# Seven-product pairs in all gate and up blocks and in six of 22 inner pairs of the down projection

## The chip, the cores and the metric

The kernel runs on one core of a Trainium2 chip. A core has TensorE (matmuls; PE in the profile), VectorE (DVE), ScalarE (ACT), GpSimd (POOL) and SyncE (SP). Each engine works through its own instructions in the order in which the program issues them, and waits on semaphores for the others. Transfers are issued from SP, ACT and POOL. The metric is the device time of one execution in microseconds; lower is better.

## The reference, cut to what matters

One encoder layer on 256 rows with model width 2048. All arithmetic is in float32. The change touches its last stage, the feed-forward block and the final norm:

```python
D_MODEL = 2048; SEQ = 256; D_FF = 5632
def swiglu(h, w_gate_up, w_down):
    gate, up = jnp.split(h @ w_gate_up, 2, axis=-1)
    return (jax.nn.silu(gate) * up) @ w_down
def reference(...):
    ...                                     # four mixers, w_out, cross attention
    x = x + swiglu(rms_norm(x, norm_g[l, 2]), w_gate_up[l], w_down[l])
    return rms_norm(x, final_norm_g)
```

Gate and up are a 256 x 2048 by 2048 x 11264 product, down a 256 x 5632 by 5632 x 2048 product.

## The kernel before, in words

**Precision.** Every float32 operand is held as a high and a low part, each in a reduced matmul format. A product of a 128-row operand with a 128 x 512 piece of weights is three matmuls: high by high, high by low, low by high (`part`, L448 to L451). The data is the stationary operand, the weights are streamed.

**The weight stream.** All weights lie in one array, cut into slabs of 128 x 2048 in the order of use. `Stream.raw` (L95) loads a slab from SP into one of three `raw` buffers (four during gate and up). `make` and `split` (L114 to L160) turn each slab into two parts of 128 x 1024: ScalarE casts the high part `wh` (L120), VectorE subtracts it from the raw slab and writes the low part `wl` (L121). `wh` and `wl` go into pools: three buffers in `wp`, two more in `wp2` during gate and up. A buffer comes free when TensorE has used its part, so VectorE and ScalarE work a few parts ahead of TensorE. `free` (L107) picks the pool; the 44 slabs of down may use `wp` alone.

**Seven products.** Two inner blocks of 128 by two column groups of 512 by two row halves of 128 make a 2 x 2 by 2 x 2 block product: eight block products, or seven with sums of blocks on both sides and additions afterwards (the scheme of Strassen and Winograd). Such a pair is called a unit; `seven` (L52) says which slabs are units. A unit's slab is split in four parts: the first of 512 columns, the others of 1024, and in between VectorE forms the weights' sums in the raw buffer (L150). `left` (L900) forms the data's sums once, `combine` (L929) adds the seven results up.

**Gate and up.** `gate_up` (L890) goes over 11 blocks j of 512 hidden columns. Each block has 8 inner pairs i of 128-blocks, for gate and up at once. `sevens` (L47) names the pairs that are units: none in block 0, (1, 5) in blocks 1 to 3, (1, 3, 5) in blocks 4 to 10. The results of the plain pairs and part of the units' results are summed in PSUM, in four banks of one of the two pools `gbank` and `bank`, which alternate by block; the other pool's four banks hold the units' four further sums. `finish` (L943) adds them, applies silu, multiplies, turns the 128 x 512 results (`store_turned`, L474) and stores them to `hidden` in DRAM by eight transfers a block from POOL (L481).

**Background work.** `combine`, `finish`, `turn`, `fetch` and others are generators in a list (`Background`). After each product the planner polls them; a step is issued only when its due time has come and VectorE owes less than 0.9 us by the planner's count. At fixed points a generator is drained, that is run to its end on the spot. So these steps' places in the engines' queues follow from how busy VectorE is by that count; a layer below may issue an instruction earlier where its inputs are ready.

**Fetch and turn.** `fetch` (L874) loads tiles of 128 x 256 of `hidden` from POOL (L882) and splits them into the operands `f` of down: the first 16 (`EARLY`) during gate and up, from block 1 on and drained after block 10; the other 28 at the start of down, six ahead. `turn` (L1007) transposes 12 of the 16 tiles of the residual on VectorE, stores them to `xrows` from POOL (L1017) and loads them back as rows.

**Down.** `down` (L1028) goes over four column groups c of 512. For each of the 44 inner blocks it takes 128 x 512 of weights and runs three matmuls for each of the two row halves into two banks. After each of the first three groups VectorE adds the residual rows (`half`, L1024), and ScalarE sums the squares. The fourth group's banks are opened with the residual by eight TensorE transposes (L1063). The last 12 inner blocks of the fourth group are held back, in tiles `held`, so that one row half ends and is normed while the other still runs. `norm` (L1039) squares the last group straight from PSUM, scales and stores the rows.

## Time and profile before

| | |
|---|---|
| median of the runs | 1467.48 us (1465.74 to 1467.96) |
| the profiled execution | 1469.45 us, of which the span is 1467.7 |
| TensorE busy | 1452.5 us (99%) |
| VectorE busy | 1105.3 us (75%) |
| ScalarE busy | 814.5 us (55%) |
| POOL busy | 161.4 us (11%) |
| weights loaded by SP | 246 transfers of 1024 KB and 11 of 512 KB |
| gate and up | about 766 to 1219 us of the span |
| down | about 1219 to 1468 us |

How to read it: the page gives busy time by engine, then 40 equal slices of the span with the busy share in tenths, then the chain that ended last. A row of groups gives source line, engine, operation, output and inputs, count, busy time, and the idle time before it with what ended it. A row of the timeline gives start, duration, engine, line, operation, tile names and shape, and in brackets the idle time before and its releaser. A row of stretches gives for each of PE, PEld (weight load), DVE, ACT and POOL the busy time and in brackets the instructions that started; then the granted TensorE clock as a share of full speed, the DMA share and GB/s. Matmuls overlap in the pipeline, so that a row's duration is longer than the distance to the next start.

### The profile page before, as it was taken

To read this page: it belongs to the slowest core of one execution; us is meant where nothing else is said; L and a number is where in the kernel's file an instruction comes from. 1 tells how busy PE (TensorE), PEld (TensorE's weight loads), DVE (VectorE), ACT (ScalarE), POOL (GpSimd) and SP (SyncE) were. 2 spreads that over 40 slices of the span, in tenths; PEclk is the share of its full clock that TensorE was granted. 3 is DMA by queue.
4 is the path that set the end of the run, shared out by engine and by line. 5 is a ranking of instruction groups with operands and counts; after the bars stand their busy time and mean duration, and the time that the engine had idled before them with its cause. 6 is when DMAs were issued, how large, how long until landed. Compare 5 with 4: busy or idle time off the path is not lost.

```text
span 1467.7 us, 19616 instructions
## 1 busy us (share of the span) xinstructions
PE 1452.5 (99%) x7275; PEld 1229.2 (84%) x7275; DVE 1105.3 (75%) x1608; ACT 814.5 (55%) x1209; POOL 161.4 (11%) x276
## 2 busy tenths in 40 slices
PE   9999999999999999999999999999999999999997
PEld 7878888898899888888888888888888888888886
DVE  6588768778867767877776788999999996544445
ACT  6556655466656556665564555565555554534344
POOL 0220100000000001110005422211101113000000
PEclk9999999999999999999999999999999999999999
DMA  9975564454636456545557866656666655655554
GB/s 349 350 256 206 201 212 168 148 185 155 212 127 209 161 200 201 183 172 186 187 201 229 284 220 212 228 201 244 221 221 244 219 203 186 241 188 188 197 200 144
DMA packets 56720, 306.11 MB, mean 209 GB/s; under 512 B 9485, under 2 KB 11182, under 8 KB 25008
## 3 DMA queue, kind: packets, MB, share of 16 engines
q1 hardware_dynamic: 45920, 281.11, 54.6%
q0 software_dynamic: 10272, 23.09, 5.3%
q8 instruction: 57, 0.93, 0.3%
q10 hardware_dynamic: 432, 0.66, 0.1%
q14 instruction: 39, 0.32, 0.1%
HBM read 291.18 MB, written 13.63 MB: 208 GB/s over the span
## 4 chain that ended last, share of the span: by engine, by line
PE 97%; DVE 1%; ACT 1%; DMA 0%; issue 0%; SPq 0%; ACTq 0%
PE pg L398 18%; PE pg L450 15%; PE pg L451 15%; PE pg L449 15%; PE pg L399 10%; PE pm L449 6%; PE pm L451 6%; PE pm L450 6%; PE pm L1180 1%; PE pg L395 1%; PE pg L396 1%; PE pm L846 1%; PE pm L819 1%; DVE wl L121 0%; DMA raw<-in_W 0%; PE pm L1560 0%
## 5 line engine op out<-in xcount | busy, mean ns | idle before, releaser
L121 DVE TENSOR_TENSOR wl<-raw,wh 128x1024 fp32r<-128x1024 f32 (+2 forms) x557 | 657.1, 1190 | 279.2 <-ACT wh L120 273.0
L120 ACT CAST wh<-raw 128x1024 fp32r<-128x1024 f32 (+2 forms) x557 | 565.5, 1023 | 517.0 <-PE pg L451 227.7
L398 PE MATMUL pg<-act,wh 128*128 128x512 f32 x1104 | 390.4, 395 | 2.9 <-DVE act L276 2.9
L399 PE MATMUL pg<-act,wl 128*128 128x256 f32 x1216 | 342.0, 281 | 0.0
L450 PE MATMUL pg<-wl,act 128*128 128x512 f32 (+1 forms) x779 | 303.2, 389 | 2.1 <-DVE wl L121 2.0
L449 PE MATMUL pg<-wh,act 128*128 128x512 f32 (+1 forms) x779 | 303.6, 390 | 0.6 <-ACT wh L120 0.5
L451 PE MATMUL pg<-wh,act 128*128 128x512 f32 (+1 forms) x779 | 303.2, 389 | 0.0
L398 PEld LDWEIGHTS pg<-act,wh 128*128 128x128 f32 x1104 | 208.8, 189 | 48.7 <-DVE act L276 3.3
L399 PEld LDWEIGHTS pg<-act,wl 128*128 128x128 f32 x1216 | 230.0, 189 | 0.8 <-DVE wl L121 0.5
L450 PEld LDWEIGHTS pg<-wl,act 128*128 128x128 f32 x779 | 146.3, 188 | 33.5 <-DVE wl L121 3.4
L449 PEld LDWEIGHTS pg<-wh,act 128*128 128x128 f32 x779 | 146.3, 188 | 32.1 <-ACT wh L120 1.2
L451 PEld LDWEIGHTS pg<-wh,act 128*128 128x128 f32 x779 | 146.2, 188 | 30.8 <-issue 0.4
L449 PE MATMUL pm<-wh,act 128*128 128x512 f32 x288 | 112.0, 389 | 0.0
L450 PE MATMUL pm<-wl,act 128*128 128x512 f32 x288 | 112.0, 389 | 0.0
L451 PE MATMUL pm<-wh,act 128*128 128x512 f32 x288 | 112.0, 389 | 0.0
L481 POOL DMA_DIRECT2D hidden<-u x88 | 56.8, 653 | 305.8 <-DVE u L478 303.7
L150 DVE TENSOR_TENSOR raw<-raw 128x512 f32<-128x512 f32 (+1 forms) x81 | 70.2, 867 | 2.1
L450 PEld LDWEIGHTS pm<-wl,act 128*128 128x128 f32 x288 | 54.1, 188 | 11.2
L449 PEld LDWEIGHTS pm<-wh,act 128*128 128x128 f32 x288 | 54.1, 188 | 11.2
L451 PEld LDWEIGHTS pm<-wh,act 128*128 128x128 f32 x288 | 54.1, 188 | 11.2
L1017 POOL DMA_DIRECT2D xrows<-tmp x48 | 27.7, 585 | 135.4 <-DVE rc L280 126.6
L276 DVE TENSOR_TENSOR tmp<-pg,tmp 128x256 f32<-128x256 f32 x78 | 32.4, 417 | 5.4 <-ACT tmp L405 4.6
(343 smaller groups left out, 1650.0 us busy)
## 6 DMA issues: line engine op xcount, KB each, us to landing
raw<-in_W SPq DMA_DIRECT2D x246, 1024.0 KB, 5.0
raw<-in_W SPq DMA_DIRECT2D x11, 512.0 KB, 7.4
hidden<-u POOLq DMA_DIRECT2D x88, 64.0 KB, 4.7
tmp<-hidden POOLq DMA_DIRECT2D x44, 128.0 KB, 5.0
res<-in_xT SPq DMA_DIRECT2D x8, 512.0 KB, 8.2
k<-in_mem SPq DMA_DIRECT2D x8, 256.0 KB, 6.7
k<-in_x SPq DMA_DIRECT2D x8, 256.0 KB, 8.7
keys<-k POOLq DMA_DIRECT2D x32, 64.0 KB, 5.0
```

The lines of the kernel that those rows point to most:

```text
L120: nc.scalar.copy(wh[:, a:b], r[:, a:b])
L121: nc.vector.tensor_tensor(out=wl[:, a:b], in0=r[:, a:b], in1=wh[:, a:b].bitcast(F32), op=ALU.subtract)
L150: op = lambda out, a, b, what=ALU.subtract: nc.vector.tensor_tensor(out=out, in0=a, in1=b, op=what)
L276: self.nc.vector.tensor_tensor(out=out, in0=a, in1=b, op=op)
L395: self.nc.tensor.matmul(p[:, 0:R], wh, slot[:, 0:R], start=start, stop=False)
L398: self.nc.tensor.matmul(p[:, :], wh, slot[:, :], start=start, stop=False)
L399: self.nc.tensor.matmul(p[:, 0:R], wl, slot[:, 0:R], start=False, stop=stop)
L449: self.nc.tensor.matmul(p, hi, wh, start=start, stop=False)
L450: self.nc.tensor.matmul(p, hi, wl, start=False, stop=False)
L451: self.nc.tensor.matmul(p, lo, wh, start=False, stop=stop)
L481: nc.gpsimd.dma_start(to[:, :, 32 * a:32 * a + 32], u[32 * a:32 * a + 32, :].rearrange("f (b t) -> f b t", t=32))
L1017: nc.gpsimd.dma_start(to[:, :, c:c + 32], u[32 * a:32 * a + 32, :].rearrange("t (b f) -> t b f", f=32))
```

## The change

- **Gate and up.** Block 0 gets one unit (pair 5), blocks 1 to 10 get three. `left` forms pair 5 first and is drained in block 0. All blocks now go through `combine` and the additions in `finish`.
- **Down.** The four column groups are taken as two groups of two. In each, inner blocks 0 to 31 are plain and the six pairs of blocks 32 to 43 are units. The plan of the first group: eight plain slabs of its first column half, then the six units alternating with plain slabs of its second half, then the last two. The second: one plain slab, seven more of the first half alternating with the six units, then eight of the second half. A plain slab is four inner blocks of one column group, 24 matmuls; a unit's slab 21.
- **Operands.** `fetch` hands the tiles of blocks 32 to 43 in pairs to `form`, which forms the data's sums on VectorE and splits them.
- **Banks.** A group of two takes all eight banks: four for the direct sums, four for the units' further sums. `combine` adds these into the residual rows in SBUF, `settle` the direct sums, then the squares.
- **Residual.** All 16 tiles are turned to rows (`turn`); the eight transposes on TensorE are gone. `norm` now adds the last bank to the rows on VectorE before the squares.
- **Pools.** One more weight buffer, `wp3`, for down up to its last unit. The operands `f` lie in a pool of their own, `held` is opened after the units.

The diff, cut to its core:

```diff
 def sevens(j):
-    return () if j == 0 else (1, 5) if j < 4 else (1, 3, 5)
+    return (1, 3, 5) if j else (5,)
+FORMED = 6
+PLAIN = FT - 2 * FORMED
+def down_plan():
+    units = [("unit", PLAIN + 2 * i) for i in range(FORMED)]
+    first, second = ([("plain", c, k) for k in range(0, PLAIN, 4)] for c in range(2))
+    mix = lambda a, b: [x for pair in zip(a, b) for x in pair] + a[len(b):]
+    one = first + [x for pair in zip(units, second) for x in pair] + second[FORMED:]
+    two = first[:1] + mix(first[1:], units) + second
+    return one, two
+PLANS = down_plan()
+DOWN = GU // 16 + 16 * DFF // 1024
+UNITS = {DOWN + i for i, x in enumerate(PLANS[0] + PLANS[1]) if x[0] == "unit"}
 def seven(slab):
     j, i = divmod(slab - GU // 16, 8)
-    return 0 <= j < DFF // 512 and i in sevens(j)
+    return slab in UNITS if slab >= DOWN else j >= 0 and i in sevens(j)
...
     def free(self, slab):
-        for pool, bufs in self.pools[:1] if slab >= NSLAB - FT else self.pools:
+        for pool, bufs, until in self.pools:
+            if slab >= until:
+                continue
             if sum(x is not None and x[0] is pool for x in self.items) < bufs:
                 return pool
...
+        slots = lambda pool, n, a, b: [pool.tile([P, 512], F32R, name=f"{n}{i}") for i in range(a, b)]
         with tc.tile_pool(name="fp", bufs=1) as fp:
             self.gap(fp, 192)
-            f = act[4:12] + [fp.tile([P, 512], F32R, name=f"f{i}") for i in range(EARLY - 8)]
+            f = act[4:12] + slots(fp, "f", 8, EARLY)
             self.gap(fp, 64)
             with tc.tile_pool(name="wp2", bufs=2) as wp2, tc.tile_pool(name="rawx", bufs=1) as st.rawx, \
                     tc.tile_pool(name="sw", bufs=1) as sw, tc.tile_pool(name="gp", bufs=1) as gp:
                 self.gap(sw, 192)
-                st.pools.append([wp2, 2])
+                st.pools.append([wp2, 2, DOWN])
                 self.gate_up(sw, gp, f)
             st.pools.pop()
             st.rawx = None
-            with tc.tile_pool(name="hp", bufs=1) as hp:
-                self.gap(hp, 192)
-                held = [hp.tile([P, 512], F32R, name=f"held{i}") for i in range(HELD // 2)]
-                self.st.places = list(zip(held[0::2], held[1::2]))
-                f += [hp.tile([P, 512], F32R, name=f"g{i}") for i in range(FT - 16 - EARLY)] + self.h3
-                self.bg.add(self.fetch(f, EARLY, FT, 6, SOON))
-                self.down(f)
-    def fetch(self, f, k0, k1, ahead, pause):
+            with tc.tile_pool(name="fq", bufs=1) as fq:
+                self.gap(fq, 192)
+                f += slots(fq, "f", EARLY, FT - 16) + self.h3
+                self.gap(fq, 64)
+                d = Down(self, f)
+                with tc.tile_pool(name="wp3", bufs=1) as wp3, tc.tile_pool(name="sd", bufs=1) as sd:
+                    self.gap(sd, 192)
+                    st.pools.append([wp3, 1, max(UNITS) + 1])
+                    d.begin(sd)
+                st.pools.pop()
+                with tc.tile_pool(name="hp", bufs=1) as hp:
+                    self.gap(hp, 192)
+                    held = [hp.tile([P, 512], F32R, name=f"held{i}") for i in range(HELD // 2)]
+                    st.places = list(zip(held[0::2], held[1::2]))
+                    d.end()
+    def fetch(self, f, k0, k1, ahead, pause, form=None):
...
             if k >= k0 + ahead:
+                i = k - ahead
+                if i >= PLAIN:
+                    if i % 2:
+                        form(i - 1, m.pop(i - 1), m.pop(i))
+                        self.have = i + 1
+                        yield pause
+                    continue
                 mark = self.mark()
-                self.split(f[k - ahead], m.pop(k - ahead))
+                self.split(f[i], m.pop(i))
                 self.keep_place(mark)
-                self.have = k - ahead + 1
+                self.have = i + 1
                 yield pause
...
-            for i in (1, 3, 5):
+            for i in (5, 1, 3):
...
-            last = None
             if j == 1:
-                self.bg.drain(forms)
                 early = self.bg.add(self.fetch(f, 0, EARLY, 3, 2.0))
...
                     if i == sevens(j)[0]:
+                        if j == 0:
+                            self.bg.drain(forms)
                         ps = [banks[1 - j % 2]() for _ in range(4)]
...
-        for i in range(12):
+        for i in range(16):
...
-        for c in range(3):
+        for c in range(4):
...
+    def form(self, k, m1, m2):
+        b = self.b
+        (a11, a21), (a12, a22) = ((x[:, 0:P], x[:, P:R]) for x in (m1, m2))
+        s = self.sd.tile([P, 512], F32, name="e", tag="e", bufs=4)[:, 0:384]
+        s2, s3, s4 = (s[:, a:a + P] for a in range(0, 384, P))
+        b.tt(s3, a11, a21, ALU.subtract)
+        b.stt(a21, a21, -1.0, a22, ALU.mult, ALU.subtract)
+        b.stt(s2, a21, -1.0, a11, ALU.mult, ALU.subtract)
+        b.tt(s4, a12, s2, ALU.subtract)
+        b.split(self.f[k], m1)
+        b.split(self.f[k + 1], m2)
+        t = self.sd.tile([P, 768], F32R, name=f"s{k}")
+        b.split2(t[:, 0:384], t[:, 384:768], s)
+        self.forms[k] = t
...
+    def plain(self, c, i, k0):
+        for k in range(k0, k0 + 4):
+            self.ready(min(FT, k + 3))
+            w = self.st.take("w_down", k, (c + i) * 512, 4)
+            if c + i == 3 and k >= PLAIN - LATE:
+                self.held.append((k, w))
+                continue
+            for r in range(2):
+                self.part((i, r), *self.whole(k, r), *w)
...
+    def unit(self, c, k):
+        self.ready(k + 2)
+        formed = lambda n: [self.forms[k][:, a + n * P:a + (n + 1) * P] for a in (0, 384)]
+        for (key, a), w in zip((("p1", self.whole(k, 0)), ((1, 0), formed(2)), ((0, 0), self.whole(k + 1, 0)),
+                                ("p5", self.whole(k, 1)), ("p7", formed(1)), ("p6", formed(0)), ((0, 1), self.whole(k + 1, 1))),
+                               self.st.take_forms("w_down", (k, k + 1), c * 512, c * 512 + 512), strict=True):
+            self.part(key, *a, *w)
...
+    def combine(self, c):
+        b, x = self.b, self.x
+        p1, p5, p7, p6 = (self.banks[n] for n in ("p1", "p5", "p7", "p6"))
+        t = lambda: self.sd.tile([P, 512], F32, name="e", tag="e", bufs=4)
+        add = lambda out, u, v: b.tt(out, u, v, ALU.add)
+        g, m = t(), t()
+        b.nc.scalar.copy(g, p1)
+        add(m, p6, g)
+        yield SOON
+        add(x(c, 0), x(c, 0), g)
+        yield SOON
+        v, w = t(), t()
+        add(v, p5, m)
+        add(m, p7, m)
+        yield SOON
+        add(w, p5, m)
+        yield SOON
+        for y, z in ((x(c + 1, 0), v), (x(c, 1), m), (x(c + 1, 1), w)):
+            add(y, y, z)
+            yield SOON
...
+    def settle(self, c, ps):
+        for r in range(2):
+            x = self.x(c, r)
+            self.b.tt(x, x, ps[r], ALU.add)
+            yield SOON
+            self.squares(x, c, r)
+            yield SOON
...
+    def begin(self, sd):
+        b = self.b
+        self.sd = sd
+        self.fetching = b.bg.add(b.fetch(self.f, EARLY, FT, 6, SOON, self.form))
+        one, two = PLANS
+        n, self.rest = (1 + max(i for i, x in enumerate(plan) if x[0] == "unit") for plan in PLANS)
+        self.open(one, b.bank)
+        self.run(0, one[:n], b.gbank)
+        todo = [b.bg.add(self.combine(0))]
+        self.run(0, one[n:n + 1], None)
+        b.bg.drain(todo[0])
+        todo.append(b.bg.add(self.settle(0, self.both(0))))
+        self.run(0, one[n + 1:], None)
+        b.bg.drain(todo[1])
+        last = b.bg.add(self.settle(1, self.both(1)))
+        self.open(two, b.gbank)
+        self.run(2, two[:1], None)
+        b.bg.drain(last)
+        self.run(2, two[1:self.rest], b.bank)
+        last = b.bg.add(self.combine(2))
+        self.run(2, two[self.rest:self.rest + 1], None)
+        b.bg.drain(last)
...
+    def norm(self, fg, r):
+        nc, ss = self.b.nc, self.ss
+        s, y, b, v, a = ss[:, 4 * r + 3:4 * r + 4], *(ss[:, 8 + 4 * r + i:9 + 4 * r + i] for i in range(4))
+        x = self.x(3, r)
+        nc.vector.tensor_tensor(out=x, in0=self.banks[1, r][:, :], in1=x, op=ALU.add)
+        self.squares(x, 3, r)
```

More of the change, by code (lines that the diff above doesn't have):

```diff
@@ L941, in combine, with finish @@
             self.tt(u1, p5, g1, ALU.add)
-        def finish(j, cs, s, last):
-            if last:
-                yield from last
+        def finish(j, cs, s):
             for r in range(2):
-                if last:
-                    self.tt(s[r][0], cs[r][0], s[r][0], ALU.add)
-                nc.scalar.activation(s[r][0], s[r][0] if last else cs[r][0], AF.Silu, scale=box["col"][:, r:r + 1])
+                self.tt(s[r][0], cs[r][0], s[r][0], ALU.add)
+                nc.scalar.activation(s[r][0], s[r][0], AF.Silu, scale=box["col"][:, r:r + 1])
                 yield SOON
@@ L953, in finish @@
                 g, h = s[r]
-                if last:
-                    self.tt(h, cs[r][1], h, ALU.add)
-                    yield SOON
+                self.tt(h, cs[r][1], h, ALU.add)
+                yield SOON
             for r in range(2):
@@ L998, in gate_up @@
                             self.bg.poll()
-            if j == 0:
-                s = [[gp.tile([P, 512], F32, name=f"{n}{r}", tag=f"{n}{r}") for n in "gh"] for r in range(2)]
-            else:
-                self.bg.drain(last)
-            end = self.bg.add(finish(j, cs, s, last))
+            self.bg.drain(last)
+            end = self.bg.add(finish(j, cs, s))
         for x in (end, turned, early):
@@ L1083, in down @@
         fg = st.rawp.tile([P, D], F32, name="raw", tag="raw")
-        nc.sync.dma_start(fg, self.t["fg"])
+        nc.sync.dma_start(fg, b.t["fg"])
         for r in range(2):
-            b, v = (ss[:, 9 + 4 * r + i:10 + 4 * r + i] for i in range(2))
-            self.stt(v, ss[:, 4 * r:4 * r + 1], EPS * D, ss[:, 4 * r + 1:4 * r + 2], ALU.add, ALU.add)
-            self.tt(v, v, ss[:, 4 * r + 2:4 * r + 3], ALU.add)
-            nc.vector.tensor_scalar(out=b, in0=v, scalar1=1.0 / D, scalar2=None, op0=ALU.mult)
+            e, v = (ss[:, 9 + 4 * r + i:10 + 4 * r + i] for i in range(2))
+            b.stt(v, ss[:, 4 * r:4 * r + 1], EPS * D, ss[:, 4 * r + 1:4 * r + 2], ALU.add, ALU.add)
+            b.tt(v, v, ss[:, 4 * r + 2:4 * r + 3], ALU.add)
+            nc.vector.tensor_scalar(out=e, in0=v, scalar1=1.0 / D, scalar2=None, op0=ALU.mult)
@@ L1090, in down @@
             for c in range(3):
-                x = self.half(c, r)
-                self.stt(x, x, 0.375, fg[:, c * 512:(c + 1) * 512], ALU.mult, ALU.mult)
+                x = self.x(c, r)
+                b.stt(x, x, 0.375, fg[:, c * 512:(c + 1) * 512], ALU.mult, ALU.mult)
         nc.scalar.mul(fg[:, 3 * 512:4 * 512], fg[:, 3 * 512:4 * 512], 0.375)
         for r in range(2):
-            for k, wh, wl in held:
-                self.part_rows(ps[r], r, f[k], wh, wl, False, k == FT - 1)
-            norm(ps[r], r)
+            for k, w in self.held:
+                self.part((1, r), *self.whole(k, r), *w)
```

108 lines of the change are left out of this document (61 added, 47 removed).

## The prediction

> **What bounds the kernel now.** I read the page's busy times first, then its slices and its chain, then the stretches of gate and up (766 to 1219 us) and of down (1220 to 1460).
>
> ```profile
> PE 1452.5 (99%) x7275; PEld 1229.2 (84%) x7275; DVE 1105.3 (75%) x1608; ACT 814.5 (55%) x1209; POOL 161.4 (11%) x276
> PE   9999999999999999999999999999999999999997
> DVE  6588768778867767877776788999999996544445
> PE 97%; DVE 1%; ACT 1%; DMA 0%; issue 0%; SPq 0%; ACTq 0%
> 766.00:810.00 44.00, 44.00 (x198) 36.51 (x197) 31.50 (x56) 22.43 (x26) 24.04 (x42) 1.00 0.73 232
> 810.00:937.00 127.00, 127.00 (x562) 105.21 (x561) 108.02 (x128) 68.14 (x80) 29.78 (x50) 1.00 0.67 234
> 937.00:1219.00 282.00, 282.00 (x1245) 233.58 (x1245) 265.78 (x297) 158.59 (x177) 43.83 (x71) 1.00 0.64 223
> 978.00:1020.00 42.00, 42.00 (x187) 34.78 (x186) 40.71 (x48) 24.05 (x29) 8.02 (x13) 1.00 0.65 230
> 1220.00:1460.00 240.00, 239.70 (x1059) 198.21 (x1057) 125.86 (x146) 106.00 (x137) 14.35 (x25) 1.00 0.57 196
> ```
>
> TensorE is the bound: 97% of the chain, and busy without a hole in all of gate, up and down. VectorE is second. In blocks 4 to 10 (937 to 1219), where three of eight inner pairs go by seven products, it is busy 265.78 of 282.00 us, in one stretch 40.71 of 42.00, and TensorE still loses nothing. In down it idles half of the time. So a product saved is worth a product's time, as long as VectorE keeps ahead.
>
> **What a matmul costs.** The busy mean of 389 ns is a pipeline's length; what counts is start to start.
>
> ```profile
> 1299.74 0.39 PE L449 MATMUL pg<-wh,f 128*128 128x512 f32 x1
> 1305.86 0.39 PE L449 MATMUL pg<-wh,g 128*128 128x512 f32 x1
> 1219.26 1.03 PE L1063 MATMUL pm<-ident,res 128*128 128x128 f32 x8
> 1220.05 0.47 PE L449 MATMUL pg<-wh,act 128*128 128x512 f32 x1
> ```
>
> Between the first two rows lie 27 steps: 6.12/27 = 0.2267 us. A product is three matmuls, 0.68 us. A pair by seven products is 21 matmuls (4.76 us) instead of 24 (5.44).
> - Gate and up: units go from 27 (six in blocks 1 to 3, 21 in 4 to 10) to 31. 4 x 3 = 12 matmuls fewer.
> - Down: 44 x 4 x 2 x 3 = 1056 matmuls become, in each of two column groups, 32 x 2 x 2 x 3 + 6 x 21 = 510, so 1020. 36 fewer.
> - Together 48 x 0.2267 = **-10.9 us**. The eight transposes that opened down go too: 1220.05 - 1219.26 = **-0.8 us**.
>
> **The tail.** The fourth column group's residual was in the PSUM bank; now VectorE adds it between the last matmul and the squares, on the path that ends the kernel.
>
> ```profile
> 1218.78 1.37 DVE L276 TENSOR_TENSOR h<-pg,h 128x512 f32<-128x512 f32 x2
> 1459.31 0.39 PE L451 MATMUL pm<-held,act 128*128 128x512 f32 x1
> 1459.73 0.58 ACT L1037 ACTIVATE pm<-pm 128x512 f32<-128x512 f32 x1 [3.85 <-PE pm L451]
> ```
>
> Such an add takes 0.68 us, with a hop to ScalarE: **+0.75 us** (0.6 to 1.0). Nothing covers it.
>
> **Gate and up: VectorE's load.** Costs again start to start, from block 8 or 9.
>
> ```profile
> 1114.78 1.22 DVE L150 TENSOR_TENSOR raw<-raw 128x1024 f32<-128x1024 f32 x1
> 1115.92 1.22 DVE L121 TENSOR_TENSOR wl<-raw,wh 128x1024 fp32r<-128x1024 f32 x1
> 1117.17 1.42 DVE L150 TENSOR_TENSOR raw<-raw 128x512 f32<-128x512 f32 x2
> 1118.51 2.50 DVE L121 TENSOR_TENSOR wl<-raw,wh 128x1024 fp32r<-128x1024 f32 x2
> 1131.71 0.69 DVE L121 TENSOR_TENSOR wl<-raw,wh 128x512 fp32r<-128x512 f32 x1 [0.32 <-ACT wh L120]
> 1132.44 1.23 DVE L150 TENSOR_TENSOR raw<-raw 128x1024 f32<-128x1024 f32 x1
> ```
>
> A slab of a unit costs 0.73 + 1.14 + 1.25 + 1.34 + 2 x 1.11 = 6.7 us of VectorE against 4.76 of TensorE; a plain slab 2 x 1.11 = 2.2 against 5.44. Four more units add 4 x 4.5 = 18 us, block 0's combining and adding 8 x 0.6 = 5, four more transposes 1.5: some 24 us. In 810 to 937 VectorE idles 19 us and in block 0 another 12, so it fits, at the utilization (97%) at which 978 to 1020 ran without a hole. I take **0** (0 to +1.5). No gain is possible there beyond the matmuls. Sixteen more row stores and two loads lie on POOL, which is busy 29.78 of 127 us: nothing.
>
> But what filled those holes was background: the splits of the first 16 hidden tiles, polled only while VectorE owes little. In the changed program's issue order only four of them (f0 to f3) are split before the last block ends. Eleven (f4 to f14) stand in VectorE's queue behind the last block's finish, and behind them stands `wl` of down's second slab, whose `wh` buffer comes free only with the last gate and up matmul.
>
> **The hand-over, worked out.** Zero is the end of the last gate and up matmul (1219.26 in this trace).
>
> ```profile
> 1220.07 1.40 DVE L280 SCALAR_TENSOR_TENSOR h<-h,rc,g 128x512 f32<-128x512 f32 x2
> 1221.39 1.29 DVE L478 STREAM_TRANSPOSE u<-h 128x512 f32<-128x512 f32 x2
> 1224.23 1.23 DVE L121 TENSOR_TENSOR wl<-raw,wh 128x1024 fp32r<-128x1024 f32 x1 [1.55 <-ACT wh L120]
> 1238.92 3.10 DVE L276 TENSOR_TENSOR g<-tmp,g 128x256 fp32r<-128x256 f32 x9
> 1241.94 1.22 DVE L121 TENSOR_TENSOR wl<-raw,wh 128x1024 fp32r<-128x1024 f32 x1
> ```
>
> Before, the transposes are through at 1222.68, +3.4. Now a 1.13 us split stands among the four adds, of which some 0.8 counts: +4.2. Eleven splits at (1241.94 - 1238.92)/9 = 0.336 make 3.7: +7.9. The weight split adds 1.22: +9.1. TensorE has one slab (24 x 0.2267 = 5.44) and one matmul before it needs it: +5.7. **A gap of about 3.5 us** (2.5 to 5). In the kernel before, the first weight split behind the finish still had 1.55 us of idle time in front of it.
>
> On POOL the loads from f15 on stand behind the last block's eight stores:
>
> ```profile
> 1223.98 3.85 POOL L481 DMA_DIRECT2D hidden<-u  x6 [0.31 <-issue]
> tmp<-hidden POOLq DMA_DIRECT2D x44, 128.0 KB, 5.0
> ```
>
> Eight at 0.64 from +4 are out at +9.4; f15 lands 5.0 us later at +14.4, and TensorE comes to it at 15 x 1.36 = +20.4 plus the gap: hidden, with 6 us and more to spare.
>
> **What a gap does to the clock.** This trace has one gap of that size.
>
> ```profile
> 479.42 0.79 PE L398 MATMUL pg<-act,wh 128*128 128x512 f32 x1 [2.94 <-DVE act L276]
> 479.40:485.40 6.00, 5.98 (x19) 5.10 (x20) 1.82 (x5) 1.00 (x2) 0.00 (x0) 0.50 0.75 262
> 485.40:491.40 6.00, 6.00 (x36) 5.29 (x36) 4.66 (x8) 4.02 (x9) 0.00 (x0) 0.98 0.06 11
> ```
>
> After 2.94 us of idling the granted clock was 0.50 for 6 us; 19 matmuls started where the next 6 us had 36: (36 - 19)/36 x 6 = 2.8 us lost on top. I add **+2.8 us** (0 to 3.5).
>
> **Down's unit stage.** From down's ninth slab units alternate with plain slabs, while the operands of the later units are still being formed. Per pair of slabs VectorE has 6.7 + 2.2, and per formed pair four 128-wide operations, two 256-wide splits and one of 384:
>
> ```profile
> 773.01 0.29 DVE L276 TENSOR_TENSOR u<-tmp 128x128 f32<-128x128 f32 x1
> 773.22 0.28 DVE L276 TENSOR_TENSOR u<-tmp,u 128x128 f32<-128x128 f32 x1
> ```
>
> That is 4 x 0.2 + 2 x 0.34 + 0.5 = 2.0, together 10.9 us against 45 x 0.2267 = 10.2 of TensorE. A lack of 0.7 over some four pairs is 2.8 us; the lead at entry, about two 1024-wide splits (2.2 us), pays for most of it. Against that, several hidden tiles are loaded only 2.5 to 4 us of TensorE work ahead of the in-order ScalarE cast or VectorE operation that waits for them, and 5.0 us (above) is what such a load takes: up to 2.4 us of blocking each, partly overlapped, with weight casts queued behind. Bounds: 0.5 (work alone) to 5 (all blocking reaches TensorE). I take the middle, **+2.5 us**. In the second column group nothing is formed any more, 8.9 against 10.2: 0; its combining is spread over plain slabs.
>
> The Trainium skill prices that load lower: "DMA: Bandwidth & Descriptors", section "Anatomy of one DMA", fits 2.0 us plus bytes/436e3, an estimate of 2.3 us for 128 KB. By it the blocking would vanish and the unit stage cost 0.5. The trace disagrees, with 5.0 us.
>
> **The sum.** The profiled execution took 1469.45 us (1.75 outside its span); the median of the runs is 1467.48, 1.97 below it. 1469.45 - 10.9 - 0.8 + 0.75 + 3.5 + 2.8 + 2.5 = 1467.3; less 1.97 it is **1465.3 us** against the median of 1467.48. Most of the 11.7 us saved on TensorE is given back in two places of down.
>
> **Rivals.** Within 0.2% (1464.5 to 1470.4) is what a measurement of this kernel can't tell from no change.
> - *The gap leaves the clock alone.* One case of 2.94 us is thin evidence. Then 1465.3 - 2.8 = 1462.5.
> - *No gap at the hand-over*, if VectorE comes through the last block faster than I count: without 3.5 and 2.8, 1459.0. Against it stands the fixed order of the queue.
> - *Slower: the unit stage drops the clock too.* If the blocking reaches TensorE in full (5 us instead of 2.5) in gaps that together count as one of 3 us, 1465.3 + 2.5 + 2.8 = 1470.6, and 1473.4 if it happens twice. For it: the lack of VectorE time. Against it: the gaps come in pieces of 1 to 2 us with matmuls between. It decides once all gaps and slow clock together pass 14 us.
> - That fewer products are run is no question; the program holds 56 fewer TensorE instructions.
>
> On the first rival the Trainium skill has a rule: "TensorE: Matmul & The Clock Gate", section "What's actually happening", has the clock halve after at least one idle window of some 3.4 us, windows running freely. By it a gap of 3.5 us would seldom hold a whole window, and 1462.5 would come out. The trace bears it out only in part: 2.94 us sufficed.
>
> **How the numbers follow.** The forecast has 0.50; its own range, with the unit stage at 0.5 to 5, is 1463.3 to 1467.8, of which 0.13 lies below 1464.5. The untouched clock has 0.20 (0.17 below), no gap 0.07, the slow unit stage 0.15. For 0.08 I have no mechanism: 0.03 below, 0.05 above. Faster 0.13 + 0.17 + 0.07 + 0.03 = 0.40; slower 0.15 + 0.05 = 0.20; the same 0.40. The range runs from the no-gap case to the first slow one: 1459.5 to 1471.
>
> **What would show it.** Right: 48 matmuls fewer at 0.2267 us; one wait of TensorE of 3 to 4 us for `wl` some 5.7 us into down; a granted clock of 0.50 for 6 us behind it; short waits for `wl` or `wh` from 50 to 85 us into down; the final squares 0.75 us later behind the last matmul. Wrong: holes in blocks 0 to 3, no wait at the hand-over, or a wait in the second column group.

## The result, and the profile after

| | before | after |
|---|---|---|
| median of the runs | 1468.05 us (13 runs) | 1465.28 us (13 runs, 1463.14 to 1467.06) |
| ratio | | 0.9981, 95% interval 0.9973 to 0.9989 |
| profiled execution, its span | 1469.45 us, 1467.7 | 1465.34 us, 1463.4 |

The time fell by 0.19%, which is inside the 0.2% that the prediction called no change, and to within 0.1 us of the forecast. First the page of the changed kernel: busy times, VectorE's slices and the shares of the chain.

```profile
PE 1443.8 (99%) x7219; PEld 1220.3 (83%) x7219; DVE 1193.2 (82%) x1748; ACT 843.3 (58%) x1250; POOL 171.6 (12%) x294
...
DVE  6588768778867767777778999999999996898875
...
PE 94%; DVE 2%; issue 1%; DMA 1%; ACT 1%; POOL 0%; SPq 0%; DVEq 0%; POOLq 0%; ACTq 0%
```

There are 56 TensorE instructions less. VectorE is at nine tenths in eleven slices of gate and up (eight before). In down it is at five to nine tenths, where it was at four and five, and 2% of the chain is now VectorE's. The timeline shows where. The first row is of the kernel before, the others of the changed one.

```profile
765.91 0.50 PE L330 MATMUL pm<-ones,acc 128*128 128x1 f32 x4
```

```profile
765.55 0.50 PE L354 MATMUL pm<-ones,acc 128*128 128x1 f32 x4
...
1216.17 0.39 PE L473 MATMUL pm<-wh,act 128*128 128x512 f32 x1
...
1220.41 1.40 DVE L300 TENSOR_TENSOR act<-tmp,act 128x256 fp32r<-128x256 f32 x4
...
1221.61 0.61 PE L473 MATMUL pm<-wh,act 128*128 128x512 f32 x2
...
1221.71 2.44 DVE L300 TENSOR_TENSOR f<-tmp,f 128x256 fp32r<-128x256 f32 x7
...
1224.06 3.50 DVE L145 TENSOR_TENSOR wl<-raw,wh 128x1024 fp32r<-128x1024 f32 x3
...
1225.34 0.50 PE L474 MATMUL pm<-wl,act 128*128 128x512 f32 x1 [3.12 <-DVE wl L145]
...
1229.33 0.39 PE L473 MATMUL pm<-wh,act 128*128 128x512 f32 x1
...
1265.36 0.49 PE L475 MATMUL pm<-wh,act 128*128 128x512 f32 x1 [1.08 <-DVE act L300]
...
1454.25 0.39 PE L475 MATMUL pg<-held,act 128*128 128x512 f32 x1
...
1454.68 0.69 DVE L1229 TENSOR_TENSOR res<-pg,res 128x512 f32<-128x512 f32 x1 [3.28 <-PE pg L475]
...
1455.40 0.60 ACT L1089 ACTIVATE pm<-res 128x512 f32<-128x512 f32 x1 [3.81 <-DVE res L1229]
```

- **Gate and up.** From the last small matmul ahead of it to the first of down it took 1216.17 - 765.55 = 450.62 us; before, 1219.26 - 765.91 = 453.35. The difference is 2.73, and 12 x 0.2267 = 2.72. There is no hole in it.
- **Hand-over.** Eleven splits (four `act`, seven `f`) stand ahead of `wl`. The next matmul was due at 1222.07 and came at 1225.34: 3.3 us.
- **Clock.** From 1225.34 to 1229.33 there are 10 steps, 3.99 us instead of 2.27: 1.7 us.
- **Tail.** From the last matmul to the end of the span it is 1463.4 - 1454.25 = 9.15 us; before, 1467.7 - 1459.31 = 8.39. So +0.76.

What the unit stage lost is read from the matmuls that start in a stretch, here 1240 to 1300 us, good to one matmul or 0.23 us. The first row is of the kernel before, the second of the changed one.

```profile
1240.00:1300.00 60.00, 60.00 (x267) 49.69 (x266) 36.38 (x50) 31.44 (x48) 8.85 (x17) 1.00 0.67 231
```

```profile
1240.00:1300.00 60.00, 58.92 (x258) 47.59 (x257) 54.14 (x92) 39.16 (x61) 9.21 (x17) 1.00 0.60 213
```

Nine matmuls less are 9 x 0.2267 = 2.0 us. The terms add up: -10.9 - 0.8 + 0.76 + 3.3 + 1.7 + 2.0 = -3.9, and with the 0.36 us by which gate and up began earlier -4.3; the spans differ by 1467.7 - 1463.4 = 4.3.

### The profile page after: what moved, and what is told of

Its sections match the earlier page's. It is cut to its first block, busy times and chain, and to the rows that moved or that the text cites. A ratio compares the mean times of both kernels' runs of the same rounds, so it can differ in the third digit from the quotient of the medians.

```text
span 1463.4 us, 19727 instructions
## 1 busy us (share of the span) xinstructions
PE 1443.8 (99%) x7219; PEld 1220.3 (83%) x7219; DVE 1193.2 (82%) x1748; ACT 843.3 (58%) x1250; POOL 171.6 (12%) x294
## 4 chain that ended last, share of the span: by engine, by line
PE 94%; DVE 2%; issue 1%; DMA 1%; ACT 1%; POOL 0%; SPq 0%; DVEq 0%; POOLq 0%; ACTq 0%
PE pg L422 19%; PE pg L474 13%; PE pg L475 13%; PE pg L473 13%; PE pg L423 10%; PE pm L475 6%; PE pm L473 6%; PE pm L474 6%; DVE wl L145 1%; PE pm L1328 1%; PE pg L419 1%; PE pg L420 1%; DMA tmp<-hidden 1%; PE pm L870 1%; PE pm L843 1%
## 5 line engine op out<-in xcount | busy, mean ns | idle before, releaser
L144 ACT CAST wh<-raw 128x1024 fp32r<-128x1024 f32 (+1 forms) x589 | 590.3, 1013 | 477.4 <-PE pg L475 154.9
L145 DVE TENSOR_TENSOR wl<-raw,wh 128x1024 fp32r<-128x1024 f32 (+1 forms) x589 | 684.1, 1178 | 185.3 <-ACT wh L144 178.6
L474 PE MATMUL pg<-wl,act 128*128 128x512 f32 (+1 forms) x689 | 268.5, 390 | 2.1 <-DVE wl L145 2.1
L473 PE MATMUL pg<-wh,act 128*128 128x512 f32 (+1 forms) x689 | 268.8, 391 | 0.0
L475 PE MATMUL pg<-wh,act 128*128 128x512 f32 (+1 forms) x689 | 268.5, 390 | 0.0
L474 PEld LDWEIGHTS pg<-wl,act 128*128 128x128 f32 x689 | 129.8, 188 | 30.1 <-DVE wl L145 3.3
L473 PEld LDWEIGHTS pg<-wh,act 128*128 128x128 f32 x689 | 129.7, 188 | 27.6 <-issue 0.8
L475 PEld LDWEIGHTS pg<-wh,act 128*128 128x128 f32 x689 | 129.7, 188 | 27.4 <-issue 0.4
L474 PE MATMUL pm<-wl,act 128*128 128x512 f32 x318 | 124.6, 392 | 3.1 <-DVE wl L145 3.1
L475 PE MATMUL pm<-wh,act 128*128 128x512 f32 x318 | 124.6, 392 | 1.1 <-DVE act L300 1.1
L473 PE MATMUL pm<-wh,act 128*128 128x512 f32 x318 | 124.1, 391 | 0.0
L174 DVE TENSOR_TENSOR raw<-raw 128x1024 f32<-128x1024 f32 x129 | 112.0, 868 | 3.0
L475 PEld LDWEIGHTS pm<-wh,act 128*128 128x128 f32 x318 | 60.1, 189 | 14.2 <-DVE act L300 1.7
L473 PEld LDWEIGHTS pm<-wh,act 128*128 128x128 f32 x318 | 60.0, 189 | 12.5
```

The lines of the kernel that those rows point to most:

```text
L144: nc.scalar.copy(wh[:, a:b], r[:, a:b])
L145: nc.vector.tensor_tensor(out=wl[:, a:b], in0=r[:, a:b], in1=wh[:, a:b].bitcast(F32), op=ALU.subtract)
L174: op = lambda out, a, b, what=ALU.subtract: nc.vector.tensor_tensor(out=out, in0=a, in1=b, op=what)
L473: self.nc.tensor.matmul(p, hi, wh, start=start, stop=False)
L474: self.nc.tensor.matmul(p, hi, wl, start=False, stop=False)
L475: self.nc.tensor.matmul(p, lo, wh, start=False, stop=stop)
```

## Experiments

| edit | median, us | ratio to before, 95% interval | gate and up to the end, us |
|---|---|---|---|
| the kernel before | 1468.05 | | 701.8 |
| the changed kernel | 1465.28 | 0.9981 (0.9973 to 0.9989) | 697.8 |
| early splits at fixed points, blocks 2 to 10 | 1460.56 | 0.9957 (0.9944 to 0.9971) | 694.9 |
| form behind the plain tiles | 1471.44 | 1.0032 (1.0020 to 1.0045) | 707.2 |
| both | 1468.10 | 1.0005 (0.9996 to 1.0014) | 704.6 |
| three units less in gate and up | 1462.80 | 0.9968 (0.9955 to 0.9980) | 696.3 |
| fixed points in blocks 5 to 10 | 1458.81 | 0.9937 (0.9923 to 0.9950) | 692.8 |
| the same, form behind, one slab ahead | 1466.54 | 0.9993 (0.9984 to 1.0002) | 699.9 |
| gate and up alone | 1469.13 | 1.0008 (0.9999 to 1.0017) | 703.3 |
| down alone | 1464.63 | 0.9983 (0.9974 to 0.9992) | 698.6 |
| down alone, form held back | 1459.69 | 0.9943 (0.9930 to 0.9955) | 693.4 |
| fixed points 5 to 10, form held back, 8 ahead | 1458.23 | 0.9934 (0.9920 to 0.9947) | 692.3 |
| the same, 10 ahead | 1459.38 | 0.9939 (0.9926 to 0.9953) | 692.8 |
| fewer splits at the hand-over | 1462.55 | 0.9965 (0.9951 to 0.9978) | 696.9 |

One caution on differences of 1 or 2 us: the stages ahead of gate and up vary from one execution to the next. The last small matmul ahead of it stood at 763.38 us in the profile with three units less and at 767.10 in that with 10 ahead. So each reason is read from its own stretch, and the last column of the table leaves the early stages out: it goes, in the one profiled execution, from that matmul to the end of the span.

```profile
763.38 0.50 PE L354 MATMUL pm<-ones,acc 128*128 128x1 f32 x4
```

```profile
767.10 0.50 PE L365 MATMUL pm<-ones,acc 128*128 128x1 f32 x4
```

### Is the hand-over gap a matter of order?

The first edit issues the splits of the early hidden tiles at two fixed points of each block, instead of when the planner finds room.

```diff
+                if j > 1 and i in (4, 6):
+                    for e in [e for e in self.bg.q if e[0] is early]:
+                        self.bg.step(e)
                 if i in sevens(j):
```

> Splits of the first 16 hidden tiles issued at two fixed points in each of blocks 2 to 10 instead of when the planner finds room; same work, other places. Theory (order of VectorE's queue makes the hand-over gap): TensorE no longer waits for wl in down's second slab, and without the gap the granted clock stays at 1.00 there. In the changed kernel the gap cost 3.3 us and the slow clock behind it 1.7, so 1465.3 - 5.0 = 1460.3 us (1459.5 to 1461.5). Rival (VectorE's load is the cause, the order only shows where): the eleven splits of 0.336 us, 3.7 us in all, come back as holes of TensorE inside gate and up, and the time stays within 1 us of 1465.3.

1460.56 us, the theory's number, but in part by luck. From the start of gate and up to the end this profile is 2.9 us shorter than the changed kernel's, not 5.0; the rest of the 4.7 lies in the early stages (763.78 us against 765.55). The timeline of this run (VectorE at the hand-over and in block 4, then TensorE in block 4):

```profile
1220.64 2.32 DVE L145 TENSOR_TENSOR wl<-raw,wh 128x1024 fp32r<-128x1024 f32 x2
966.61 0.45 DVE L1050 STREAM_TRANSPOSE tmp<-res 128x256 f32<-128x256 f32 x1 [3.25 <-DMA xrows<-tmp]
977.82 0.50 PE L474 MATMUL pm<-wl,act 128*128 128x512 f32 x1 [1.71 <-DVE wl L145]
```

`wl` now stands right behind the transposes, at 1220.64 instead of 1224.06, and TensorE waits for nothing at the hand-over. There is a new wait of 1.71 us in block 4, which cost 2.0 start to start and gave back that much of the gain. Its cause is not VectorE's load: VectorE stood 3.25 us because the forced loads took the `tmp` buffers that the turning of the residual needs. The next edit leaves the blocks alone in which the residual is turned.

```diff
-                if j > 1 and i in (4, 6):
+                if j > 4 and i in (2, 4, 6):
```

> Early splits at three fixed points in each of blocks 5 to 10 only. In the run with fixed points from block 2 on, the forced loads took the tmp buffers that the turning of the residual needs; VectorE stood 3.25 us behind an xrows store and TensorE lost 1.9 us at 977.8 us. Turning ends at about 900 us when nothing is forced. Theory (that hole is the buffers', not VectorE's load): no wait of TensorE from 766 to 1255 us, 1460.6 - 1.9 = 1458.7 us. Rival (VectorE at 97% has no room for the splits in blocks 5 to 10): a hole or holes of 1 to 2 us come back there, 1460 to 1461 us.

1458.81 us, again the theory's number, and from gate and up on 692.8 us instead of 697.8: the 5.0 that gap and slow clock cost. The only wait of TensorE listed between 766 and 1460 us is the one of the unit stage (1.2 us for `act`). So VectorE does have room for the 16 splits in blocks 5 to 10. The gap was one of the planner's order: it issues these splits only when VectorE owes little by its count. That count itself was not recorded.

The other way to give room is to take work away, three units of blocks 1 to 3:

```diff
-    return (1, 3, 5) if j else (5,)
+    return (5,) if j == 0 else (1, 5) if j < 4 else (1, 3, 5)
```

> Gate and up blocks 1 to 3 go back to two units (28 instead of 31), down as changed. Nine matmuls more at 0.2267 us: +2.0 us. Theory: VectorE has room in blocks 1 to 3, all 16 hidden tiles are split in time, the hand-over gap and the slow clock go: -5.0, in sum 1465.3 - 3.0 = 1462.3 us. Rival (gap has another cause, such as the weight stream or the buffers changing over): gap stays, 1467.3 us.

1462.80 us. The gap is gone, as the theory said, but the unit stage lost more than in the changed kernel: 251 matmuls in the stretch from 1240 to 1300 us, 16 x 0.2267 = 3.6 us instead of 2.0.

```profile
1240.00:1300.00 60.00, 57.52 (x251) 46.43 (x250) 56.67 (x92) 36.77 (x53) 4.34 (x8) 1.00 0.55 193
```

### The two parts of the change alone

Gate and up alone is the kernel before with `sevens` and `gate_up` of the changed one; down alone is the changed kernel with those two of the kernel before.

```diff
 # gate and up alone, against the kernel before
-    return () if j == 0 else (1, 5) if j < 4 else (1, 3, 5)
+    return (1, 3, 5) if j else (5,)
...
-            for i in (1, 3, 5):
+            for i in (5, 1, 3):
```

> The kernel before with gate and up as changed (31 units), down as before. Theory: 12 matmuls less are 2.7 us; twelve splits of hidden tiles still stand in VectorE's queue behind the last block, the eight transposes (0.8 us) shorten the wait for wl a little: gap of 2.9 and slow clock of 1.7 us. 1467.6 - 2.7 + 4.6 = 1469.5 us (1468 to 1471): slower than before. Rival (the gap belongs to down's new buffers and operands): 1467.6 - 2.7 = 1464.9 us.

```profile
1220.58 2.76 DVE L276 TENSOR_TENSOR f<-tmp,f 128x256 fp32r<-128x256 f32 x8
1223.27 3.48 DVE L121 TENSOR_TENSOR wl<-raw,wh 128x1024 fp32r<-128x1024 f32 x3
1224.53 0.80 PE L450 MATMUL pg<-wl,act 128*128 128x512 f32 x1 [2.53 <-DVE wl L121]
```

1469.13 us against 1469.5 expected: the gap belongs to the units of gate and up, not to down's buffers. Alone, this part gives its whole 2.7 us back. By the profiles it is 1.5 us slower from gate and up on (703.3 against 701.8); by the medians that is inside the noise.

> Down as changed, gate and up as before (27 units). Theory: 36 matmuls are 8.2 us, the transposes 0.8, the tail gives back 0.6, no gap at the hand-over, in the unit stage 1.2 to 2.5 us of waits: 1467.6 - 8.2 - 0.8 + 0.6 + 1.2 = 1460.4 us (1460 to 1462). Rival (the gap belongs to down's new buffers): 1465.4 us.

1464.63 us, 4 us more than expected. There is no gap at the hand-over, but the unit stage lost 5 us: 243 matmuls instead of 267, 24 x 0.2267 = 5.4. What ScalarE and VectorE waited for from 1222 to 1262 us in this run:

```profile
ACT act L308 <- DMA tmp<-hidden: 7.5, 2, 4.2
DVE act L300 <- ACT act L308: 3.1, 1, 3.1
```

The two waits of ScalarE in its timeline, with what follows the first:

```profile
1242.51 0.41 ACT L308 CAST act<-tmp 128x256 fp32r<-128x256 f32 x1 [4.22 <-DMA tmp<-hidden]
1242.82 1.05 ACT L144 CAST wh<-raw 128x1024 fp32r<-128x1024 f32 x1
1250.70 0.41 ACT L308 CAST act<-tmp 128x256 fp32r<-128x256 f32 x1 [3.32 <-DMA tmp<-hidden]
```

A cast of a formed tile stood for its load, with the next weight part queued behind it, and VectorE behind both. In the program's order most of form's casts stand 2.3 to 4 us of TensorE work behind the issue of their loads, and a load takes 4.7 us to landing in this run (5.1 in the changed kernel). The next edit keeps form's operations behind the split of the tile three before, and those of later pairs behind the pair two before; `behind` adds, for each instruction since the mark, an order dependency on the last instruction of the same engine ahead of that point:

```diff
...
                     if i % 2:
+                        mark = self.mark()
                         form(i - 1, m.pop(i - 1), m.pop(i))
+                        self.behind(mark, self.ends[min(i - 3, PLAIN - 1) if i < PLAIN + 4 else i - 4])
+                        self.ends[i] = self.mark()
...
                 self.keep_place(mark)
+                self.ends[i] = self.mark()
```

> As the run with down alone changed, but the operations of form may not stand ahead of the split of the tile three before (from the third formed pair on: of the pair two before), so that each stands 7 us of TensorE work and more behind the load that it needs instead of 2.3 to 4. Theory (the 5 us that the unit stage lost are ScalarE and VectorE blocked by loads of hidden tiles, 7.5 and 3.1 us, with weight parts queued behind): these waits go and most of the 5.0 us with them, 1464.6 - 4 = 1460.6 us (1459.6 to 1462). Rival (VectorE has too much to do there, 10.9 us for a pair of slabs against 10.2): the loads' waits go but TensorE still waits for wl, 1463 to 1465 us.

1459.69 us, 4.9 less. The same two stretches of down alone, and then with form held back:

```profile
1240.00:1300.00 60.00, 56.30 (x243) 44.97 (x243) 53.08 (x87) 36.02 (x53) 4.44 (x9) 1.00 0.52 185
1262.00:1282.00 20.00, 16.54 (x70) 12.53 (x69) 20.00 (x33) 12.52 (x17) 0.00 (x0) 1.00 0.38 133
```

```profile
1240.00:1300.00 60.00, 60.00 (x267) 49.67 (x266) 57.47 (x95) 37.72 (x55) 4.90 (x9) 1.00 0.60 214
1262.00:1282.00 20.00, 20.00 (x90) 16.57 (x89) 20.00 (x32) 12.91 (x17) 0.00 (x0) 1.00 0.58 208
```

VectorE is busy 20.00 of 20 us in both. With the loads' waits gone TensorE starts 90 matmuls there instead of 70, as many as it can. So it was blocking by loads that brought the unit stage's loss about. In down alone TensorE's waits in the second stretch are for `wl` (3.4 us): the loads had used up VectorE's lead, and a VectorE that is never idle could not win it back. Where the lead was kept, it cost nothing that VectorE has more to do there than TensorE by the prediction's count.

### The unit stage of the whole change

An earlier try at the same place kept all of form strictly behind whatever is issued ahead of it:

```diff
+        mark = b.mark()
         (a11, a21), (a12, a22) = ((x[:, 0:P], x[:, P:R]) for x in (m1, m2))
...
         self.forms[k] = t
+        b.keep_place(mark)
```

> The forming of the unit's data sums stays behind the plain tiles' splits in ScalarE's and VectorE's queues. Theory (order again: the last plain tile's split stands behind form's operations in the queue): the wait of TensorE for act in L475 at 1265 us of the span, 1.24 us with its start to start, goes, and 1465.3 - 1.2 = 1464.1 us. Rival (VectorE's load: it is busy without a hole from 1268 to 1290): the formed operands now come too late for the first units, the hole moves there, no change or up to 2 us more. The hand-over gap stays as it is in both.

> Both edits of order: early splits at fixed points and form behind the plain tiles. Theory: the two gains add, 1465.3 - 5.0 - 1.2 = 1459.1 us, with no wait of TensorE over 0.5 us from 766 us on. Rival: without the pause at the hand-over TensorE reaches the units 3.5 to 5 us earlier against the same VectorE and the same 5.0 us loads of hidden tiles, so that a part of the 5 us comes back as holes in the unit stage: 1461 to 1464 us.

Both were slower than theory and rival said, at 1471.44 and 1468.10 us. What TensorE waited for in the first of them:

```profile
PE pg L473 <- ACT act L308: 6.7, 5, 2.1
```

The 1.08 us wait at the last plain tile is gone, but `form` is asked for only when its unit is due, so five of the six units now waited for their own operands. Calling it one slab ahead, on top of the fixed points in blocks 5 to 10:

```diff
-            self.ready(min(FT, k + 3))
+            self.ready(min(FT, k + (5 if k >= PLAIN - 4 else 3)) if c + i == 0 else 0)
...
             self.unit(c, x[1])
+            self.ready(min(FT, x[1] + 4))
```

> As the run before, and form stays behind the plain tiles but is called one slab ahead of its unit. Theory (the unit stage's wait is one of order): the last plain tile's split comes in time, the formed operands too: no wait over 0.5 us in down, 1458.7 - 1.2 = 1457.5 us. Rival (VectorE's load: 10.9 us for a pair of slabs against 10.2 of TensorE): TensorE waits for wl or act at the units all the same, 1 to 3 us in sum, 1458.5 to 1460.5 us.

```profile
1263.25 0.50 PE L473 MATMUL pg<-wh,act 128*128 128x512 f32 x1 [1.56 <-ACT wh L144]
1297.22 0.50 PE L474 MATMUL pg<-wl,act 128*128 128x512 f32 x1 [1.24 <-DVE wl L145]
1321.30 0.49 PE L474 MATMUL pg<-wl,act 128*128 128x512 f32 x1 [1.71 <-DVE wl L145]
```

1466.54 us, worse than even the rival said: now the weight parts behind form were late, at three units. Holding form back by a fixed distance (the edit made in down alone) and asking for the hidden tiles earlier did better; the second run has `k + 10` in place of `k + 8`:

```diff
-            self.ready(min(FT, k + 3))
+            self.ready(min(FT, k + 8 if c + i == 0 else 0))
```

> As the run with fixed points in blocks 5 to 10, with form behind as in the run beside it, and the hidden tiles asked for eight ahead of their use instead of three. Theory: the waits of ScalarE and VectorE for hidden tiles (4.2 and 1.2 us) go, the 2.0 us lost in down before the first unit go: 1458.8 - 2.0 = 1456.8 us (1456.3 to 1457.8). Rival (VectorE's load): the hole moves behind the first unit, 1458 to 1461 us.

> As the run with fixed points in blocks 5 to 10 and form held back, with the hidden tiles asked for ten ahead of their use instead of eight, which puts VectorE's operations in down in nearly the order that ran without a hole with down alone changed. Theory (the last 1.2 us of holes are order): no wait of TensorE over 0.2 us in down, 1458.2 - 1.1 = 1457.1 us (1456.2 to 1458). Rival (VectorE, which comes out of blocks 5 to 10 with more behind it than with 27 units, is short by about that much): 1458 to 1459 us.

1458.23 and 1459.38 us. The stretch from 1240 to 1300 us with eight ahead, and with ten ahead:

```profile
1240.00:1300.00 60.00, 59.52 (x261) 48.34 (x261) 57.90 (x94) 36.69 (x55) 4.20 (x8) 1.00 0.58 211
```

```profile
1240.00:1300.00 60.00, 59.35 (x259) 47.90 (x258) 56.35 (x91) 37.09 (x55) 4.80 (x9) 1.00 0.56 202
```

They lost 1.4 and 1.8 us there, where the fixed points alone lost 2.3 (257 matmuls) and down alone with form held back lost none. So both went the rival's way, the second even past its 1459: with 31 units in gate and up, holes that add up to 1 to 2 us stay in the unit stage. That VectorE enters it with less lead than with 27 units is likely, but was not tested by itself. The two fastest, 1458.23 and 1458.81, can't be told apart; both beat the kernel before by 0.6% and, by their ratios to it, the changed one by some 0.45%.

### How large a gap halves the clock

One fixed point in each of blocks 6 to 10 leaves seven `f` splits at the hand-over:

```diff
+                if j > 5 and i == 4:
+                    for e in [e for e in self.bg.q if e[0] is early]:
+                        self.bg.step(e)
```

> The changed kernel with one fixed point in each of blocks 6 to 10: seven instead of eleven splits stand ahead of wl at the hand-over. The gap should be 3.3 - 4 x 0.336 = 1.9 us. So far waits of 1.7 and 1.8 us left the clock at 1.00, waits of 2.1 and more halved it for 3.3 us. Theory (TensorE idle for more than some 2 us halves the clock): no drop at the hand-over, 1465.3 - 1.35 - 1.76 = 1462.2 us. Rival (any gap over 1.8 us): the drop stays, 1463.9 us.

The timeline, and two stretches with the granted clock third from the end:

```profile
1223.97 0.50 PE L474 MATMUL pm<-wl,act 128*128 128x512 f32 x1 [2.11 <-DVE wl L145]
```

```profile
1222.10:1225.40 3.30, 1.43 (x6) 1.20 (x7) 3.30 (x6) 0.45 (x1) 3.30 (x7) 1.00 0.74 128
1225.50:1228.90 3.40, 3.40 (x10) 2.63 (x9) 1.07 (x2) 1.04 (x1) 3.10 (x6) 0.50 0.87 327
```

The gap came out at 2.11 us, not 1.9, and the clock did halve. (The expectation counts a wait of 1.8 us among those that left the clock at 1.00; the trace of that run shows the opposite, see the last section.) The time, 1462.55, is nearer to the number given for no drop, but the clock is not the reason: with gap and drop the profiled span is 1462.1, 1.3 below the changed kernel's, of which the shorter gap makes 1.0. The rest lies in what the early stages vary by. This profile is of the slowest of the four executions (1464.20 us); whether the clock fell in the other three, no profile shows. The last section puts this case beside the others.

## Why the prediction was right

- **Matmuls, -10.9; transposes, -0.8; tail, +0.75.** Right: -2.73 in gate and up, the tail +0.76, and the sum of the terms closes on the spans.
- **Gate and up: VectorE's load, 0.** Right: no hole. VectorE even took the early splits at fixed points in blocks 5 to 10 without one.
- **Hand-over gap, +3.5.** Right in place and cause: `wl` was forecast to be through 9.1 us after the last gate and up matmul, 1216.17 + 9.1 = 1225.3, and the matmul came at 1225.34. The size is 3.3. Moving the splits removed it twice; the units of gate and up alone brought it about.
- **Clock after the gap, +2.8.** The mechanism was right, the term mis-sized: 1.7. It was taken from one case, the gap of 2.94 us at 479 us, with 6 us and more at 0.50. Here the clock was low for 3.4 us. The rival that the gap leaves the clock alone did not come, but that is in part luck: in the run with three units less the same 2.94 us at 479 us did leave the clock alone (last section).
- **Unit stage, +2.5.** 2.0. Of its two reasons one held. Blocking by loads of hidden tiles is real, and in down alone it cost the 5 us that were its upper bound. The lack of VectorE time, 0.7 us for a pair of slabs, cost nothing in down alone once the blocking was taken away; with 31 units in gate and up, 1.4 us or more of holes stayed, whose cause is open. The forecast waits "for `wl` or `wh`" were one wait of 1.08 us for `act`, the last plain tile's split, behind form's operations.
- **No gap at the hand-over**, the rival at 1459.0, is what two of the experiments made: 1460.56 and 1458.81.
- **The slow unit stage**, the rival at 1470.6, did not come. From 1222 to 1262 us ScalarE waited 1.8 us for such loads (row below), against 7.5 in down alone and 4.2 with fixed points in blocks 5 to 10. It was not the pause of the gap that spared the changed kernel that loss: without the gap, and with 31 units, the unit stage still lost only 2.3 us (fixed points in blocks 5 to 10), against 5.4 in down alone. What did, perhaps a later fetching by the planner, was not separated. A clock that falls in the unit stage did come up, in the two runs with form strictly behind, after gaps of 2.1 us; but those were late operands, not blocked casts.

```profile
ACT act L308 <- DMA tmp<-hidden: 1.8, 2, 1.4
```

- **The basis.** The measured terms give -3.9 us, the forecast's gave -2.15; the mis-sized ones (0.2, 1.1 and 0.5) are the difference. The medians of the 13 runs each show -2.8. The 1.1 us between -3.9 and -2.8 is a matter of which execution was profiled: the 1469.45 us of the kernel before lie above all 13 of its runs (highest 1469.42), the 1465.34 us of the changed one at its median. That the forecast came within 0.1 us owes something to this and to the median of three runs that it started from, 0.6 below that of 13.

The Trainium skill's page "DMA: Bandwidth & Descriptors", section "Anatomy of one DMA", gives 2.3 us for such a load, an estimate by its fit, by which the blocking would vanish. The trace showed 5.1 us after the change too, and the run with form held back shows that the difference is real time: 4.9 us came back when the casts stood further behind the loads.

## What to carry to other kernels

Work that a planner fits into idle time has no place of its own: when the other work grows, it does not slow down, it piles up at the next point where it is drained, in front of whatever stands behind that point, so give it a place. When an in-order engine is moved ahead to meet its inputs, count with the landing time that the trace shows, since one cast that waits for a load holds up all weights behind it. And read a busy engine by whether the bound engine waits for it: VectorE ran at 20.00 of 20 us both where TensorE lost nothing and where it lost a fifth.

## What was not expected of the hardware

The granted clock changes on a fixed grid. In all 14 profiles the falls and rises of one execution from 476 us on lie multiples of 3.41 us apart, to within the 0.1 us of the reading. In the changed kernel it fell at 478.2 and 1225.7 us, and 747.5/3.413 is 219.0; it rose at 485.1 and 1229.2. The stretches between (granted clock third from the end):

```profile
478.20:485.10 6.90, 5.85 (x18) 4.98 (x19) 2.85 (x7) 1.16 (x3) 0.00 (x0) 0.51 0.68 228
1222.30:1225.60 3.30, 0.26 (x1) 0.26 (x2) 3.30 (x8) 1.01 (x2) 3.30 (x6) 1.00 0.48 101
1225.70:1229.10 3.40, 3.40 (x10) 2.63 (x9) 1.86 (x2) 0.00 (x0) 3.40 (x7) 0.51 0.90 294
1229.20:1232.60 3.40, 3.40 (x17) 2.77 (x16) 1.23 (x1) 1.36 (x2) 1.79 (x4) 1.00 1.00 389
```

So the price of a gap comes in steps: one interval of 3.41 us at half clock costs 1.7 us, two cost 3.4. In the changed kernel's profile the gap at 479 us cost two, that at the hand-over one. In the run with form strictly behind the gap at the hand-over was as long (3.11 us) but lay otherwise on the grid, and the clock was low for two:

```profile
1221.10:1224.40 3.30, 0.98 (x5) 0.47 (x3) 3.30 (x10) 2.07 (x3) 3.30 (x6) 1.00 0.48 99
1224.50:1231.20 6.70, 6.01 (x14) 4.76 (x15) 2.90 (x3) 1.02 (x1) 5.41 (x11) 0.50 0.87 292
```

The gap that suffices is shorter than the one that the prediction knew. A gap of 1.71 us in block 4 (first edit) left the clock at 1.00. A gap of 1.80 us at the same place, in the run with both edits, halved it:

```profile
975.80:979.10 3.30, 1.50 (x7) 0.96 (x6) 3.30 (x5) 1.21 (x2) 1.08 (x2) 1.00 0.86 264
979.20:982.50 3.30, 3.30 (x9) 2.61 (x8) 3.30 (x5) 0.64 (x1) 3.30 (x6) 0.50 0.80 219
```

All seven gaps of 1.80 to 3.12 us from gate and up on halved the clock, and each filled at least 53% of one interval; no gap up to 1.71 us, half an interval, did.

The gap at 479 us, which every profile has at 2.94 or 2.95 us, shows that the length alone does not decide; the place on the grid does too. It cost two intervals in three of the 14 profiles (the kernel before among them, from which the prediction took its one case), one in ten, and none in the run with three units less. There it ended at 479.69 us, and the grid, counted back from the fall at the end of the kernel, has its borders at 477.93 and 481.35: the gap filled 35% of one interval and 51% of the next. In the other 13 profiles it filled 56% or more of one. The run with three units less, its gap and the clock in the two intervals behind it:

```profile
479.69 0.50 PE L422 MATMUL pg<-act,wh 128*128 128x512 f32 x1 [2.94 <-DVE act L300]
477.90:481.30 3.40, 1.61 (x9) 1.45 (x10) 2.74 (x6) 1.04 (x4) 0.00 (x0) 1.00 0.27 43
481.40:484.80 3.40, 3.40 (x21) 3.01 (x20) 1.87 (x3) 2.39 (x5) 0.00 (x0) 1.00 0.96 377
```

By this the gap of 3.1 us at the hand-over could have cost nothing, one interval or two, as it fell on the grid. That an interval idle for more than about half is what counts fits all these gaps, but no run was made for that alone.

The Trainium skill has the interval: "TensorE: Matmul & The Clock Gate", section "What's actually happening", gives a free-running window of 3413 ns, and the grid agrees. It says that the clock halves after at least one idle window. Here a gap of 1.80 us was enough, so an interval need not be idle throughout.
